# Expert tables loaded in pairs of tiles, and the gates of PEER spilled by 32 tokens

## The chip, the cores and the metric

One core of a Trainium2 chip runs the whole layer. The metric is the device time in us of one execution; several executions give a median. The engines are PE (matmul), DVE (vector), ACT (scalar), POOL (GpSimd, which issues the indirect gathers), SP (which issues nearly all other DMAs) and 16 DMA engines that all queues share.

## The reference

A layer with 512 tokens of 1024 channels: attention with a sliding window and a causal pooling branch, merged by gates, then PEER, a retrieval over 16384 single-neuron experts, then a last RMSNorm. What the change touches is PEER:

```python
q = (xc @ w_query).reshape(c, 8, 2, 128)
sc = einsum('chpd,hpkd->chpk', q, sub_keys)           # 16 score sets of 128 keys
sv, si = lax.top_k(sc, 16)
cand = sv[:, :, 0, :, None] + sv[:, :, 1, None, :]    # 256 candidates a head
fv, fi = lax.top_k(cand.reshape(c, 8, 256), 16)
idx = take_along_axis(cidx, fi, -1); g = softmax(fv)  # expert number = 128*i + j
a = gelu(einsum('chkd,cd->chk', u_tab[idx], xc))
out = einsum('chk,chkd->cd', g * a, v_tab[idx])
```

All arithmetic is in float32.

## The kernel before

**Two ways for PEER.** Block 0 of 128 tokens (GB) gathers its rows of the u and v tables with indirect DMAs, two for each of the 128 choices of a token (`gather`, L735): POOL issues, DVE forms the dot product (L745) or adds the row (L749). The other 384 tokens (three blocks, ND) go through both tables densely: for each of 128 tiles n of 128 experts, `u_part` (L604) forms gelu(u tile times tokens), a gate matrix says how much each token wants of each expert, and `v_mm` (L630) adds gates times v tile into PSUM. Of the first block of those, 32 tokens (CT) have their u side by gathers too (`few`, L716), so a u tile is multiplied with 352 tokens.

**Precision.** Each matmul is three: ACT casts a float32 tile to `wh` (L121, or `vh`), DVE forms the rest `wl` = raw - wh (L113, or `vl`), and PE multiplies hi by hi, hi by lo and lo by hi (L108 to L110). So each weight tile of 512 KB passes DMA, ACT, DVE, PE. The raw tiles `wr` have RAW = 3 buffers, filled by SP in program order; a load waits until DVE has done the `low` that last read its buffer. In the dense phase the v tiles use `vr`, also 3 buffers.

**Stages** (us in the profile of before). Mixing and its projections run to 356. `scores` (L446) to 470: 16 tiles of `w_query`, of 24 matmuls 128x512 each, `match` after each, and after four of them a block of `top16` on DVE, 80 instructions (L486 to L494) for 4 projections of 4 blocks of tokens; after every fourth projection comes one `u_part`. DVE's order in this stage, `top16` against `low`, is made by a scheduler. Then the route to 978: `part()` (L825) runs u tiles ahead of time, 104 in all, of which 14 results stay in SBUF (RES) and 90 are written to `ahead`; beside them run by credits (R_A, G_A a part) the top 16 of the candidates (`select`, L496), the one-hot work and the gathers. `onehot` (L556) makes the gates: a batch is 8 tokens; `ohj` is made on ACT for 3 batches of 4 (8 times L574 and once L575) and on DVE for the fourth (L577), `ohi` on DVE (L580, L581), PE multiplies them (L590), ACT copies the product to `gs` (L591), and after TG = 16 tokens `gs` goes to `spill` in HBM in one DMA of 1 MB (L593). There are three spreads of 16 batches: one at 658 to 742, two at 797 to 978. Six more parts (TAIL) cover the first loads of the dense phase.

**The dense phase** (`dense`, L674) takes 128 iterations, from 1004 to 1657. Each loads a v tile (512 KB, L120), reloads the 176 KB result of a u tile (`gar`, L619), and in four of every eight iterations a quarter of the gates of the next eight tiles (`gt`, L627, 384 KB in runs of NI * TG * 4 = 512 bytes). ACT and DVE make `wh`, `wl` and `vh`, `vl`; PE does 18 matmuls 128x512. The last 24 iterations, from 1434, do their u part in place: a u tile more and 24 matmuls 128x352. The remaining gather rows are spread over the phase, at a rate G_B / G_V three times higher an iteration in the last 24. The order of PE, DVE and ACT is as the program is written here; SP's and POOL's DMAs follow by their waits.

Of the kernel before, what the change touches and what calls it, by code (L numbers as in the profile page):

```python
# [19 lines left out]
P = 128  # L20
# [20 lines left out]
GB = 0  # L41
# [5 lines left out]
TG = 16  # L47
# [3 lines left out]
G_A = 1.0  # L51
# [7 lines left out]
RES = 14  # L59
SC = 1.4  # L60
RAW, ROWS, WB = 3, 4, 3
OHN, OHA = 4, 3


class Layer:
# [49 lines left out]
    def weights(self, src, pool=None, tag="w", late=False):  # L115
        k = WB if pool is None else 2
        pool = pool or self.w
        raw, hi, lo = (pool.tile([P, D], t, name=tag + n, tag=tag + n, bufs=b)
                       for n, t, b in (("r", F32, RAW), ("h", F32R, k), ("l", F32R, k)))
        self.nc.sync.dma_start(out=raw, in_=src)  # L120
        self.nc.scalar.copy(hi, raw)  # L121
# [277 lines left out]
    def residual(self, wp, tp, mg, xn2, nat):  # L399
# [5 lines left out]
        def load(k):  # L405
            raw = self.w.tile([P, D], F32, name="wr", tag="wr", bufs=RAW)
# [197 lines left out]
    def u_part(self, n, w, xn2, keep=False):  # L604
        ps = self.project(w, xn2, slice(DB * P + CT, DB * P + TD))
        if keep and n < RES:
            ga = self.held[n] = self.ga.tile([P, TU], F32, name=f"gk{n}", bufs=1)
# [3 lines left out]
        if keep and n >= RES:  # L611
            self.nc.sync.dma_start(out=self.ahead[n], in_=ga)
        return ga

    def reload(self, n):
        if n < RES:
            return self.held.pop(n)
# [37 lines left out]
    def v_load(self, m):  # L655
        self.vs[m], low = self.weights(self.a["v_experts"][m * P:(m + 1) * P, :], self.dp, "v", late=True)
        return low
# [16 lines left out]
    def dense(self, ahead, xn2, acc, fetch):  # L674
        us = {}

        def u_load(m):
            if ahead <= m < NKEY:
                us[m] = self.weights(self.a["u_blocks"][m])
# [101 lines left out]
    def run(self):  # L781
        nc, tc, a = self.nc, self.tc, self.a
        xn2 = self.pair(self.x, "x")
        with tc.tile_pool(name="merged", bufs=1) as self.m:
# [4 lines left out]
            nat = {GB: self.c.tile([P, D], F32, name="natg")}  # L789
            self.cp = self.pool("few", 1, side="right")  # L790
            self.natc = self.cp.tile([P, D], F32, name="natc")
# [4 lines left out]
        with tc.tile_pool(name="route", bufs=1, reuse_waits="tile") as tp:  # L796
            subk = tp.tile([P, 16, P], F32, name="subk")
            nc.scalar.dma_start(out=subk, in_=a["sub_keys"])

# [23 lines left out]
            self.held = {}  # L823
# [10 lines left out]
            for i, _ in enumerate(self.scores(xn2, tp, sv, si, subk)):  # L834
                if i % U_S == U_S - 1:
                    part()
# [11 lines left out]
        with tc.tile_pool(name="dense", bufs=2, reuse_waits="tile") as self.dp:  # L848
# [13 lines left out]
            for c in range(ND):  # L862
                hb = dp.tile([P, D], F32, name="hb", tag="vr", bufs=RAW)
# [68 lines left out]
```

## Time and profile before

| | us |
|---|---|
| three runs | 1670.08, 1674.9 (median), 1680.72 |
| profiled execution, its own time | 1678.21 |
| its span in the profile | 1676.4 |
| busy in the span: PE, DVE, ACT, POOL | 1578.3, 1285.2, 803.8, 371.4 |
| DMA | 417.83 MB, mean 249 GB/s |

PE is busy for 94% of the span, but the stages have different limits, so the window rows by stage say more than this mean. A matmul's busy time overlaps its neighbours', so the distance between starts is the better measure of PE's pace. [...]

### The profile page before, as it was taken

To read this page: it belongs to the slowest core of one execution; us is meant where nothing else is said; L and a number is where in the kernel's file an instruction comes from. 1 tells how busy PE (TensorE), PEld (TensorE's weight loads), DVE (VectorE), ACT (ScalarE), POOL (GpSimd) and SP (SyncE) were. 2 spreads that over 40 slices of the span, in tenths; PEclk is the share of its full clock that TensorE was granted. 3 is DMA by queue.
4 is the path that set the end of the run, shared out by engine and by line. 5 is a ranking of instruction groups with operands and counts; after the bars stand their busy time and mean duration, and the time that the engine had idled before them with its cause. 6 is when DMAs were issued, how large, how long until landed. Compare 5 with 4: busy or idle time off the path is not lost.

```text
span 1676.4 us, 23543 instructions
## 1 busy us (share of the span) xinstructions
PE 1578.3 (94%) x8389; PEld 1370.7 (82%) x8389; DVE 1285.2 (77%) x2379; ACT 803.8 (48%) x1434; POOL 371.4 (22%) x302
## 2 busy tenths in 40 slices
PE   7999999999998989899888989999999999999997
PEld 6777788888898989889888887777877778787876
DVE  4676434437899999789888858888887888788887
ACT  4655533333343436983998943333333333332334
POOL 0000000000001243223322213243333333254550
PEclk9999999999999989999999999999999999999999
DMA  6211222532236888878878799999999999999994
GB/s 213 65 62 64 75 95 94 184 117 93 84 114 224 276 293 294 283 259 266 297 274 288 260 303 371 335 354 365 366 364 336 342 356 361 331 332 358 333 334 154
DMA packets 173175, 417.83 MB, mean 249 GB/s; under 512 B 15616, under 2 KB 88064, under 8 KB 169856
## 3 DMA queue, kind: packets, MB, share of 16 engines
q1 hardware_dynamic: 130576, 262.65, 45.3%
q0 software_dynamic: 41728, 151.05, 26.0%
q10 hardware_dynamic: 752, 2.62, 0.4%
q8 instruction: 66, 1.08, 0.3%
q14 instruction: 53, 0.43, 0.1%
HBM read 370.12 MB, written 45.06 MB: 248 GB/s over the span
## 4 chain that ended last, share of the span: by engine, by line
PE 41%; issue 23%; DMA 11%; ACT 9%; DVE 8%; POOL 7%; SPq 1%; POOLq 0%; DVEq 0%; ACTq 0%
PE mm L108 7%; PE mm L109 7%; PE mm L110 7%; POOL row L712 7%; PE acc L109 4%; PE acc L108 4%; PE acc L110 4%; DMA row<-v_experts,ei 3%; DMA vr<-v_experts 3%; ACT ohj L574 3%; ACT gs L591 2%; DVE wl L113 2%; ACT wh L121 1%; PE ho L108 1%; PE ho L110 1%
## 5 line engine op out<-in xcount | busy, mean ns | idle before, releaser
L108 PE MATMUL mm<-xh,wh 128*128 128x352 f32 (+2 forms) x1424 | 491.2, 345 | 11.3 <-ACT ga L610 8.0
L110 PE MATMUL mm<-xh,wl 128*128 128x352 f32 (+2 forms) x1424 | 483.7, 340 | 6.2 <-DVE wl L113 6.2
L109 PE MATMUL mm<-xl,wh 128*128 128x352 f32 (+2 forms) x1424 | 483.6, 340 | 0.7 <-DVE xl L113 0.7
L712 POOL DMA_INDIRECT row<-u_experts,ei x128 | 158.3, 1237 | 847.3 <-ACT ga L610 528.3
L113 DVE TENSOR_TENSOR wl<-wr,wh 128x1024 fp32r<-128x1024 f32 x187 | 228.3, 1222 | 143.8 <-ACT wh L121 138.9
L108 PE MATMUL acc<-vh,wh 128*128 128x512 f32 x768 | 303.5, 395 | 19.7 <-ACT wh L650 12.8
L121 ACT CAST wh<-wr 128x1024 fp32r<-128x1024 f32 x187 | 195.6, 1046 | 245.6 <-PE mm L109 188.8
L109 PE MATMUL acc<-vl,wh 128*128 128x512 f32 x768 | 304.0, 396 | 7.7 <-DVE vl L113 7.4
L110 PE MATMUL acc<-vh,wl 128*128 128x512 f32 x768 | 302.9, 394 | 0.0
L108 PEld LDWEIGHTS mm<-xh,wh 128*128 128x128 f32 x1424 | 271.0, 190 | 32.1 <-ACT ga L610 10.3
L110 PEld LDWEIGHTS mm<-xh,wl 128*128 128x128 f32 x1424 | 270.8, 190 | 21.6 <-DVE wl L113 7.8
L109 PEld LDWEIGHTS mm<-xl,wh 128*128 128x128 f32 x1424 | 271.2, 190 | 13.8 <-DVE xl L113 1.1
L650 ACT CAST wh<-wf 128x384 fp32r<-128x384 f32 x128 | 65.7, 514 | 363.0 <-PE acc L109 174.0
L712 POOL DMA_INDIRECT row<-v_experts,ei x128 | 163.7, 1279 | 308.1 <-DVE hg L749 268.4
L113 DVE TENSOR_TENSOR vl<-vr,vh 128x1024 fp32r<-128x1024 f32 x128 | 156.5, 1223 | 69.1 <-ACT vh L121 63.2
L108 PEld LDWEIGHTS acc<-vh,wh 128*128 128x128 f32 x768 | 145.3, 189 | 55.9 <-ACT wh L650 16.6
L109 PEld LDWEIGHTS acc<-vl,wh 128*128 128x128 f32 x768 | 145.4, 189 | 45.4 <-DVE vl L113 16.7
L110 PEld LDWEIGHTS acc<-vh,wl 128*128 128x128 f32 x768 | 145.3, 189 | 34.3 <-DVE wl L113 4.4
L749 DVE SCALAR_TENSOR_TENSOR hg<-row,act,hg 128x1024 f32<-128x1024 f32 x128 | 163.9, 1281 | 4.0 <-DMA row<-v_experts,ei 3.5
L745 DVE SCALAR_TENSOR_TENSOR row<-row,natg 128x1024 f32<-128x1024 f32 x128 | 156.0, 1219 | 6.8 <-DMA row<-u_experts,ei 6.8
L121 ACT CAST vh<-vr 128x1024 fp32r<-128x1024 f32 x128 | 134.0, 1047 | 52.6 <-DMA vr<-v_experts 48.1
L590 PE MATMUL pg<-ohi,ohj 128*128 128x128 f32 x768 | 96.5, 279 | 27.5 <-ACT ohj L575 24.2
(188 smaller groups left out, 1743.7 us busy)
## 6 DMA issues: line engine op xcount, KB each, us to landing
wr<-u_blocks SPq DMA_DIRECT2D x128, 512.0 KB
vr<-v_experts SPq DMA_DIRECT2D x128, 512.0 KB
spill<-gs SPq DMA_DIRECT2D x24, 1024.0 KB
gt<-spill SPq DMA_DIRECT2D x64, 384.0 KB
ahead<-ga SPq DMA_DIRECT2D x90, 176.0 KB
gar<-ahead SPq DMA_DIRECT2D x90, 176.0 KB
wr<-w_in SPq DMA_DIRECT2D x30, 512.0 KB
wr<-w_query SPq DMA_DIRECT2D x16, 512.0 KB
```

The lines of the kernel that those rows point to most:

```text
L108: mm(out, lhsT=l[0], rhs=r[0], start=first, stop=False)
L109: mm(out, lhsT=l[0], rhs=r[1], start=False, stop=False)
L110: mm(out, lhsT=l[1], rhs=r[0], start=False, stop=last)
L113: self.lowered = self.nc.vector.tensor_tensor(lo, src, hi.bitcast(F32), op=ALU.subtract).ins
L121: self.nc.scalar.copy(hi, raw)
L574: nc.scalar.activation(ohj[:, z, :], self.iota, AF.Abs, bias=tr[:, 1, u + z:u + z + 1])
L590: nc.tensor.matmul(pg[:, z, :], lhsT=ohj[:, z, :], rhs=ohi[:, z, :], start=True, stop=True)
L591: nc.scalar.copy(gs[0][:, :, t0:t0 + 8].rearrange("p i t -> p t i"), pg)
L650: nc.scalar.copy(wh, wf)
L712: self.nc.gpsimd.indirect_dma_start(out=t, out_offset=None, in_=tab, in_offset=bass.IndirectOffsetOnAxis(ap=ei[:, s:s + 1], axis=0))
L745: nc.vector.scalar_tensor_tensor(u, u, 1.0, xn2, op0=ALU.mult, op1=ALU.mult, accum_out=act[:, s:s + 1])
L749: nc.vector.scalar_tensor_tensor(z, v, act[:, s:s + 1], z, op0=ALU.mult, op1=ALU.add)
```

## The change

- **Tables in pairs.** Two neighbouring u tiles, and two v tiles, come in one DMA of 1 MB, 8192 contiguous bytes a partition instead of 4096 (`u_tile`, `v_tile`). For v, a pair holds the experts with j even and odd next to each other, so `indices` maps an expert to another tile and row: 3 tensor_scalar and 1 tensor_tensor instead of 2 tensor_scalar. The u table comes to the kernel as `u_pairs`, laid out so.
- **Buffers.** `wr` has 2 buffers of 8 KB a partition instead of 3 of 4 KB, for every stream; a single tile (`w_in`, `w_o`, `w_query`) fills half of one. `vr` likewise has 2 pairs.
- **Gates.** TG is 32: `gs` goes to HBM every 4 batches in 2 MB, and `gt` comes back in runs of 1024 bytes, in the same 64 loads of 384 KB.
- **One-hot.** `ohj` is made on ACT for every second batch (OHN, OHA = 2, 1): L574 issues 192 instead of 288, L575 24 instead of 36, L577 24 instead of 12.
- **Smaller things.** G_A is 1.1: 62 gather rows of block 0 are asked for ahead of the dense phase instead of 51, so 194 instead of 205 are left for it. KEEP and HELD keep 2 + 12 u results in SBUF, as many as RES, but those of the u parts 2 and 3 go to `ahead`. `score`'s tiles are in a pool of their own, and `natg` is in another pool.

The instructions of PE keep their number (7819); 104 parts ahead, 90 of them written to `ahead`, and 24 in the dense phase stand in both.

The core of the diff:

```diff
-TG = 16
+TG = 32
-G_A = 1.0
+G_A = 1.1
-RES = 14
+KEEP = 2
+HELD = 12
-RAW, ROWS, WB = 3, 4, 3
-OHN, OHA = 4, 3
+RAW, ROWS, WB = 2, 4, 3
+OHN, OHA = 2, 1
...
+    def raw(self):
+        return self.w.tile([P, 2, D], F32, name="wr", tag="wr", bufs=RAW)
+
+    def weights(self, src):
+        raw = self.raw()[:, 0, :]
         self.nc.sync.dma_start(out=raw, in_=src)
+        return self.halves(raw, self.w, "w", WB)
...
+    def u_tile(self, m):
+        if m % 2 == 0:
+            self.two_u = self.raw()
+            self.nc.sync.dma_start(out=self.two_u.rearrange("p j d -> p (j d)"), in_=self.a["u_pairs"][m // 2])
+        return self.halves(self.two_u[:, m % 2, :], self.w, "w", WB)
+
+    def v_tile(self, m):
+        if m % 2 == 0:
+            self.two_v = self.dp.tile([P, 2, D], F32, name="vr", tag="vr", bufs=2)
+            self.nc.sync.dma_start(out=self.two_v.rearrange("p j d -> p (j d)"), in_=self.a["v_pairs"][m // 2])
+        return self.halves(self.two_v[:, m % 2, :], self.dp, "v", 2, late=True)
...
-        v.tensor_scalar(ij[:, 0, :], ei, 7, None, op0=ALU.arith_shift_right)
-        v.tensor_scalar(ij[:, 1, :], ei, NKEY - 1, None, op0=ALU.bitwise_and)
+        v.tensor_scalar(ij[:, 1, :], ei, 1, None, op0=ALU.bitwise_and)
+        v.tensor_scalar(ij[:, 0, :], ei, 8, 1, op0=ALU.arith_shift_right, op1=ALU.logical_shift_left)
+        v.tensor_tensor(ij[:, 0, :], ij[:, 0, :], ij[:, 1, :], op=ALU.bitwise_or)
+        v.tensor_scalar(ij[:, 1, :], ei, 1, NKEY - 1, op0=ALU.arith_shift_right, op1=ALU.bitwise_and)
...
             def part():
                 nonlocal ahead
                 with tc.high_priority(HP):
-                    w = self.weights(a["u_blocks"][ahead])
+                    w = self.u_tile(ahead)
...
+    a["v_pairs"] = a["v_experts"].rearrange("(m p j) d -> m p (j d)", p=P, j=2)
```

The buffers change the order in which SP loads the tiles of `scores`. SP before, from the end of the `w_o` projection (names: `wr` a raw tile, `hb`, `hspill` and `natc` blocks of the residual):

```order
L120 DMA wr_2981<-w_query 128x1024
L427 DMA hspill<-hb_2686 128x1024
L120 DMA wr_3106<-w_query 128x1024
L120 DMA wr_3145<-w_query 128x1024
L120 DMA wr_3182<-w_query 128x1024
L120 DMA wr_3218<-u_blocks 128x1024
L120 DMA wr_3252<-w_query 128x1024
```

SP in the change, from the load of the first pair of u tiles:

```order
L135 DMA wr_2950<-u_pairs 128x2048
L444 DMA hspill<-hb_2686 128x1024
L121 DMA wr_2984<-w_query 128x1024
L121 DMA wr_3109<-w_query 128x1024
L121 DMA wr_3148<-w_query 128x1024
L121 DMA wr_3185<-w_query 128x1024
L121 DMA wr_3253<-w_query 128x1024
```

The pair is loaded ahead of tile 4 of `w_query`, and its second half is read only by the u part that stands after tile 7. Until then its buffer is held, and the tiles 4 to 7 (rows 3 to 6) share the other one. The same comes again with the second pair and the tiles 12 to 15.

DVE's order moves with it. DVE before, in the first block of `top16` (`sv`, `si` values and indices, `sc` scores):

```order
L486 MAX sv_2734<-sc 128x8 x4
L488 MAX_INDEX si_2738<-sv_2734,sc 128x8 x4
L490 MATCH_REPLACE sc<-sv_2734,sc 128x128
L113 TENSOR_TENSOR wl<-wr,wh 128x1024
L490 MATCH_REPLACE sc<-sv_2734,sc 128x128 x3
L492 MAX sv_2734<-sc 128x8 x4
```

DVE in the change, the last of four equal parts of that block and what stands behind it:

```order
L503 MAX sv_2734<-sc 128x8 x4
L505 MAX_INDEX si_2738<-sv_2734,sc 128x8 x4
L507 MATCH_REPLACE sc<-sv_2734,sc 128x128 x4
L509 MAX sv_2734<-sc 128x8 x4
L511 MAX_INDEX si_2738<-sv_2734,sc 128x8 x4
L114 TENSOR_TENSOR wl<-wr,wh 128x1024 x6
```

The rest `wl` of tile 7, which stood inside the first block, now stands behind all 80 instructions of it, as the first of six; the third block has no `wl` inside either, where it had two.

SP in the dense phase before, one group of gates:

```order
L120 DMA vr<-v_experts 128x1024
L627 DMA gt<-spill 128x6x128
L619 DMA gar<-ahead 128x352
L627 DMA gt<-spill 128x6x128
L120 DMA vr<-v_experts 128x1024
L619 DMA gar<-ahead 128x352
L627 DMA gt<-spill 128x6x128
L120 DMA vr<-v_experts 128x1024
L619 DMA gar<-ahead 128x352
L627 DMA gt<-spill 128x6x128
L120 DMA vr<-v_experts 128x1024
```

and in the change, the same group:

```order
L141 DMA vr<-v_experts 128x2048
L639 DMA gar<-ahead 128x352
L647 DMA gt<-spill 128x3x256
L639 DMA gar<-ahead 128x352
L647 DMA gt<-spill 128x3x256 x2
L141 DMA vr<-v_experts 128x2048
L639 DMA gar<-ahead 128x352
L647 DMA gt<-spill 128x3x256
L639 DMA gar<-ahead 128x352
L141 DMA vr<-v_experts 128x2048
```

Before, at most two gate loads stood ahead of a v load of 512 KB; now three stand ahead of a v load of 1 MB.

## Rows read from the trace of the kernel before

**Rows 1.** The head of the page: the span of the profiled execution.

```profile
span 1676.4 us, 23543 instructions
```

**Rows 2.** Windows, one row for each stage of the program that the prediction prices: start and end in us, length, then the busy us and number of instructions of PE, PEld, DVE, ACT and POOL, the granted TensorE clock, the DMA share and GB/s.

```profile
356.00:470.00 114.00, 113.55 (x619) 99.86 (x619) 80.44 (x405) 37.88 (x56) 0.00 (x0) 1.00 0.27 93
...
470.00:658.00 188.00, 175.87 (x1061) 173.35 (x1060) 180.20 (x577) 74.28 (x109) 42.24 (x36) 0.96 0.73 245
...
658.00:742.00 84.00, 73.86 (x523) 70.67 (x523) 70.32 (x104) 78.42 (x138) 19.79 (x13) 1.00 0.78 272
...
797.00:978.00 181.00, 160.97 (x1132) 155.78 (x1132) 149.11 (x145) 171.79 (x301) 43.87 (x28) 1.00 0.81 277
...
1004.00:1434.00 430.00, 415.66 (x1789) 335.14 (x1788) 351.90 (x477) 159.89 (x302) 138.24 (x118) 0.99 1.01 355
...
1434.00:1657.00 223.00, 209.84 (x1053) 181.31 (x1053) 188.23 (x229) 77.41 (x137) 99.93 (x80) 0.99 0.91 319
```

**Rows 3.** Timeline of DVE through `scores`: start, duration, line, operation, out<-in, shapes, and in brackets the idle time before it. L486 is the first instruction of a block of `top16`, L113 the rest of a weight tile, L504 the first instruction of `select`.

```profile
387.85 0.87 DVE L486 MAX8 sv<-sc 128x8 f32<-128x128 f32 x4
...
394.61 1.21 DVE L113 TENSOR_TENSOR wl<-wr,wh 128x1024 fp32r<-128x1024 f32 x1
...
407.70 2.34 DVE L113 TENSOR_TENSOR wl<-wr,wh 128x1024 fp32r<-128x1024 f32 x2
...
446.38 0.87 DVE L486 MAX8 sv<-sc 128x8 f32<-128x128 f32 x4
...
470.26 0.87 DVE L486 MAX8 sv<-sc 128x8 f32<-128x128 f32 x4
...
494.65 0.27 DVE L504 CAST sf<-si 128x256 f32<-128x256 uint32 x1
```

**Rows 4.** Timeline of PE in `scores`: the first matmul behind the products of a score block that reads the rest (`wl`) of a weight tile.

```profile
399.76 0.39 PE L110 MATMUL mm<-xh,wl 128*128 128x512 f32 x1
```

**Rows 5.** The chain that ended last: pieces of it that are DMAs, with start us, duration us, and what was moved. `wr<-u_blocks` and `vr<-v_experts` are 512 KB each, `spill<-gs` 1 MB.

```profile
776.09 5.35 DMA wr<-u_blocks
...
904.85 3.48 DMA wr<-u_blocks
...
978.30 5.80 DMA spill<-gs
...
1071.97 11.32 DMA vr<-v_experts
```

**Rows 6.** Windows of 4 us on both sides of a stall of PE in the route, columns as in rows 2.

```profile
600.00:604.00 4.00, 3.77 (x24) 3.48 (x22) 2.55 (x12) 1.17 (x1) 0.94 (x1) 1.00 1.03 411
...
616.00:620.00 4.00, 4.00 (x15) 4.00 (x14) 4.00 (x6) 0.00 (x0) 1.68 (x1) 0.50 0.87 263
```

**Rows 7.** Groups of instructions in the one-hot stretch from 797 to 978 us: line, engine, operation, out<-in, shapes, count, busy us in all, mean ns of one, idle time before them and its releaser; and the summary of the tile `gs` in the same stretch, with the first and the last start of its 32 copies.

```profile
L591 ACT COPY gs<-pg 128x1024 f32<-128x1024 f32 x32 | 63.0, 1996 | 6.9 <-PE pg L590 6.9
...
L574 ACT ACTIVATE ohj<-iota,tr 128x128 f32<-128x128 f32 x192 | 59.5, 401 | 4.5 <-DVE tr L564 4.5
...
L575 ACT ACTIVATE ohj<-ohj 128x1024 f32<-128x1024 f32 x24 | 25.6, 1065 | 0.3
...
L577 DVE TENSOR_TENSOR ohj<-iota,tr 128x1024 f32<-128x1024 f32 x8 | 9.8, 1222 | 6.9 <-PE pg L590 6.9
...
L749 DVE SCALAR_TENSOR_TENSOR hg<-row,act,hg 128x1024 f32<-128x1024 f32 x14 | 17.9, 1279 | 0.0
...
L591 ACT COPY gs<-pg x32: 1929/1997/2057, 807.3 to 976.3; 128x1024 f32<-128x1024 f32 x32
```

**Rows 8.** DMA queues by window: packets, MB, and the time of the packets as a share of 16 DMA engines over the window. First 350 to 375 us, where q1 moves 4096-byte packets of `w_query` tiles but for 64 of 2 KB or less and q10 moves `sub_keys` in 8192-byte packets.

```profile
q1 hardware_dynamic: 576, 2.10, 24.0%
...
q10 hardware_dynamic: 144, 1.05, 10.8%
```

**Rows 9.** The same view from 990 to 996 us, where q1 moves mostly the 512-byte runs of `gt`; then 1004 to 1434 us, with the number of issues of `vr` and `gt` under it; then 1434 to 1657 us. q0 is the queue of the indirect gathers.

```profile
q1 hardware_dynamic: 2545, 1.30, 80.4%
...
q1 hardware_dynamic: 67304, 89.47, 60.6%
q0 software_dynamic: 17295, 62.96, 39.9%
...
vr<-v_experts SPq DMA_DIRECT2D x100, 512.0 KB
...
gt<-spill SPq DMA_DIRECT2D x49, 384.0 KB
...
q0 software_dynamic: 11520, 41.95, 53.9%
```

**Rows 10.** GB/s in 40 equal slices of the window from 0 to 25 us, in which the loads of x and `w_in` run with nothing beside them (4096-byte packets).

```profile
GB/s 0 0 52 190 328 262 249 367 328 413 420 419 420 419 420 419 349 325 179 5 40 76 120 178 268 357 403 413 426 420 419 275 203 79 236 354 243 0 92 328
```

**Rows 11.** Timeline of PE in the two parts of the dense phase: 128x512 products of the v table, 17 products from the first row to the second, and 128x352 products of a u tile, 23 from the third row to the fourth.

```profile
1099.76 0.39 PE L109 MATMUL acc<-vl,wh 128*128 128x512 f32 x1
...
1103.61 0.39 PE L108 MATMUL acc<-vh,wh 128*128 128x512 f32 x1
...
1502.01 0.33 PE L108 MATMUL mm<-xh,wh 128*128 128x352 f32 x1
...
1505.67 0.32 PE L110 MATMUL mm<-xh,wl 128*128 128x352 f32 x1
```

**Rows 12.** Waits from 1004 to 1434 us: who waited <- for what: us in all, times, longest us.

```profile
ACT vh L121 <- DMA vr<-v_experts: 40.9, 21, 5.5
```

More of the change, by code (lines that the diff above doesn't have):

```diff
@@ L113, in low, with halves @@
         self.lowered = self.nc.vector.tensor_tensor(lo, src, hi.bitcast(F32), op=ALU.subtract).ins
[L115 to L119, printed above, removed]
+    def raw(self):
+        return self.w.tile([P, 2, D], F32, name="wr", tag="wr", bufs=RAW)
+    def weights(self, src):
+        raw = self.raw()[:, 0, :]
         self.nc.sync.dma_start(out=raw, in_=src)
+        return self.halves(raw, self.w, "w", WB)
+    def halves(self, raw, pool, tag, bufs, late=False):
+        hi, lo = (pool.tile([P, D], F32R, name=tag + n, tag=tag + n, bufs=bufs) for n in "hl")
         self.nc.scalar.copy(hi, raw)
@@ L405, in load @@
         def load(k):
-            raw = self.w.tile([P, D], F32, name="wr", tag="wr", bufs=RAW)
+            raw = self.raw()[:, 0, :]
             nc.sync.dma_start(out=raw, in_=self.a["w_o"][k])
@@ L605, in u_part @@
         ps = self.project(w, xn2, slice(DB * P + CT, DB * P + TD))
-        if keep and n < RES:
-            ga = self.held[n] = self.ga.tile([P, TU], F32, name=f"gk{n}", bufs=1)
+        if keep and self.room:
+            self.room -= 1
+            ga = self.held[n] = self.home.tile([P, TU], F32, name=f"gk{n}", bufs=1)
         else:
@@ L610, in u_part @@
         self.nc.scalar.activation(ga, ps, AF.Gelu)
-        if keep and n >= RES:
+        if keep and n not in self.held:
             self.nc.sync.dma_start(out=self.ahead[n], in_=ga)
@@ L615, in reload @@
     def reload(self, n):
-        if n < RES:
+        if n in self.held:
             return self.held.pop(n)
@@ L655, in v_load @@
     def v_load(self, m):
-        self.vs[m], low = self.weights(self.a["v_experts"][m * P:(m + 1) * P, :], self.dp, "v", late=True)
+        self.vs[m], low = self.v_tile(m)
         return low
@@ L678, in u_load @@
             if ahead <= m < NKEY:
-                us[m] = self.weights(self.a["u_blocks"][m])
+                us[m] = self.u_tile(m)
         def rate(m):
@@ L788, in run @@
             self.psum(self.ctx, "ps3", 3)
-            nat = {GB: self.c.tile([P, D], F32, name="natg")}
             self.cp = self.pool("few", 1, side="right")
+            nat = {GB: self.cp.tile([P, D], F32, name="natg")}
             self.natc = self.cp.tile([P, D], F32, name="natc")
@@ L795, in run @@
         self.rows = self.pool("rows", ROWS, reuse_waits="tile")
-        with tc.tile_pool(name="route", bufs=1, reuse_waits="tile") as tp:
-            subk = tp.tile([P, 16, P], F32, name="subk")
-            nc.scalar.dma_start(out=subk, in_=a["sub_keys"])
+        with tc.tile_pool(name="route", bufs=1, side="right", reuse_waits="tile") as tp:
             def pool(b):
@@ L822, in run @@
             ahead = 0
-            self.held = {}
+            self.held, self.home, self.room = {}, self.ga, KEEP
             def part():
@@ L832, in part @@
                 return after
-            for i, _ in enumerate(self.scores(xn2, tp, sv, si, subk)):
-                if i % U_S == U_S - 1:
-                    part()
+            with tc.tile_pool(name="score", bufs=1, side="right", reuse_waits="tile") as sp:
+                subk = sp.tile([P, 16, P], F32, name="subk")
+                nc.scalar.dma_start(out=subk, in_=a["sub_keys"])
+                for i, _ in enumerate(self.scores(xn2, sp, sv, si, subk)):
+                    if i % U_S == U_S - 1:
+                        part()
+            self.home, self.room = self.pool("held", 1, reuse_waits="tile"), HELD
             first = Background(self.select(tp, sv[GB], si[GB], ei[GB], gw[GB]))
@@ L862, in run @@
             for c in range(ND):
-                hb = dp.tile([P, D], F32, name="hb", tag="vr", bufs=RAW)
+                hb = dp.tile([P, 2, D], F32, name="hb", tag="vr", bufs=2)[:, 0, :]
                 nc.sync.dma_start(out=hb, in_=self.hspill[c])
```

2 lines of the change are left out of this document (1 added, 1 removed).

## The prediction

> **What bounds the kernel now.** I read the table of windows by stage first, since a mean over the span mixes unlike stages. The sum is made against the profiled execution's own time of 1678.2 us (span 1676.4 [rows 1]); the median of the three runs is 3.3 us lower. Five stages are touched [rows 2]. In `scores` (356 to 470) PE is busy 113.55 of 114 us: PE bounds it. From 470 to 658 DVE is busy 180.2 of 188 us: DVE bounds the selection. In the one-hot stretch from 797 to 978 ACT is busiest, 171.79 of 181 us, with PE at 160.97 and DVE at 149.11; 658 to 742 reads alike (78.42 of 84, then 73.86 and 70.32). In the dense phase to 1434 the DMA share is 1.01, PE 415.66 of 430; from 1434 to 1657 the share is .91.
>
> For the dense phase I also take PE's pace. Seventeen products of 128x512 take 3.85 us from start to start, so eighteen, an iteration, 4.08; 23 products of a u tile take 3.66 us, so 24 take 3.82 [rows 11]. The 1789 matmuls to 1434 are 99.4 iterations, 405 us of 430: about 25 us are lost, 2.0 in each group of eight iterations. The 1053 from there on are 25.1 iterations of 7.90 us, 198 of 223: another 25 lost. That is all that faster transfers can give back there. In the first part the losses are ACT's: 40.9 us of waiting for `vr` in 21 waits [rows 12].
>
> **Scores: the loss.** Raw tiles have two buffers now, and a pair of u tiles holds one of them while four tiles of `w_query` go through the other, each load behind DVE's `low` of the tile ahead. A load takes about 3.5 us (chain pieces: 3.48 and 5.35 [rows 5]). DVE's order fell in with this: `low` of tile 7 ran at 394.61, inside the first block of `top16`, which lasted from 387.85 to 407.70 [rows 3]; now it stands behind the block. Without that one instruction (1.13 us of spacing, from 1.21 busy) the block takes 18.7 us, so the `low` runs at 406.6 and ends at 407.8. PE wants it where it read `wl` at 399.76 [rows 4]: 7 to 8 us of stall, and behind it the whole queue of PE. Then tiles 8 to 11 follow from late loads, and the second block of `top16`, which needs tile 11, starts about 7 us late. Tiles 12 to 14 each take load, cast and `low` through one buffer, 3.5 + 1.07 (as the ACT operation of the same shape, L575 [rows 7]) + 1.2 us, and start only when the second block is done: I get the third block at 457 instead of 446.38. Tile 15's `low` stands behind its 18.7 us, at 476.5; PE's pass, 24 x .2265 = 5.4 us, and ACT's copies come after it, so the fourth block starts at about 486.6 instead of 470.26. It holds two `low`s where before it held five (24.39 us to 494.65), so `select` starts at 507.7: **+13 us**. What could cover it is gone: the stage behind it is DVE's. Bounds: 8, if the first stall alone stays, and 20, if the stalls also cost clock; behind an earlier stall in the route the granted clock fell from 1.00 to .50, which is 1.2 GHz of the two levels [rows 6].
>
> Elsewhere two raw buffers mean at most a wait in the mixing, where tiles are asked for two ahead: **+1** (0 to 4).
>
> **More rows in the route.** Eleven more gathered rows come before the dense phase. A row costs DVE 1.28 us [rows 7]; some 6.5 of the eleven fall in the selection, bound by DVE, 8 us; most of the four others and all of POOL's issues lie beside PE. Part of the eight fills DVE's gaps: **+5** (0 to 9).
>
> **One-hot: the gain.** A batch costs ACT 24 of 32 times (59.5 + 25.6) / 24 = 3.55 us for `ohj`, and DVE the other times 1.22 [rows 7]. With 16 of 32 on each, ACT falls by 8 x 3.55 = 28.4 to 143.4 us in 797 to 978, DVE rises by 9.8 to 158.9, PE stays at 161. In 658 to 742 ACT falls by 14.2, DVE rises by 4.9 to 75.2. The bounds go from 172 to 161 and from 78.4 to 75.2, and if the stretches shrank to their busiest engine it would be 20 + 8.8, so 28 us in all. Batches come every (976.3 - 807.3) / 31 = 5.45 us now; 161 us over 32 batches would be 5.03. But PE and DVE would then stand within 2% of each other, and neither covers the other's waits, so I take half: **-14** (-28 to 0, the latter if PE's waits for ACT only turn into waits for DVE). The new integer instructions on 128x128 are few: four more a block, well under 1 us each, counted in this range.
>
> **The joint.** The last spill is 2 MB; one of 1 MB took 5.80 us on the chain [rows 5], and the first gate loads wait for it: **+1** (-1 to +5), since six u parts lie beside it.
>
> **Dense phase.** Priced in time of 16 engines. A packet of 4096 bytes took 24.0% x 25 x 16 / 512 = 187 ns (512 such packets make the 2.10 MB), one of 8192 took 10.8% x 25 x 16 / 128 = 337 ns, so 169 for 4 KB [rows 8]: 100 v loads of 128 packets save 128 x 100 x 18 / 16 = 14 us (0 if the rate in a full queue doesn't move). A run of 512 bytes took 80.4% x 6 x 16 / 2545 = 30.3 ns [rows 9]; 49 loads of 768 are 71 us. At the 4 KB rate per byte it would be 23.4 ns, or 55 us: no row has 1024 bytes, so I take the middle, -8 (-16 to 0). Six rows fewer: 62.96 MB of gathers are 120 rows, 39.9% of 430 us, 1.43 us each, -9. In all -31 of some 434 us, which would put the DMA under PE's 405. As the losses come in bursts behind the gate loads, I give back two thirds of the 25: **-17** (-25 to -5). In the last part 4.6 rows less at 53.9% x 223 / 80 = 1.50 us are -7, pairs -7, gates -1; two thirds of 15: **-10** (-24 to 0).
>
> On the gates a rule speaks against this. By the Trainium skill (DMA: Bandwidth & Descriptors, Specifications) a transfer runs at line rate from 512 bytes on, so doubling the runs would give nothing there; by it the term of -8 is 0. The row of 30.3 ns against 23.4 for the same bytes at 4 KB disagrees, if the mix of that window is not the reason.
>
> **Sum:** 1 + 13 + 5 - 14 + 1 - 17 - 10 = -21, so 1657 against 1678.2, and **1654** against the median.
>
> **Rivals.**
> *The serial loads are hidden and the dense phase reaches PE's pace.* The loads of tiles 4 to 7 may be early enough, as PE's order has been moved too, and then `scores` costs nothing; and the first dense part gives 25 instead of 17. 1654 - 13 - 8 = 1633. Against it: the `low` of tile 7 is behind the block by program order whatever the loads do. Chance .15.
> *Packets change nothing.* In a full queue the memory sets the rate; then only the rows saved count, 9/31 of the first term (-5) and 7/15 of the second (-5): 1654 + 12 + 5 = 1671. For it: 355 GB/s at a share of 1.01 in the dense phase. Against: 413 to 420 GB/s with 4096-byte packets at the start [rows 10]. Chance .21. The Trainium skill (HBM Reference, Specifications (TRN2)) gives a core about 358 GB/s with both cores of a pair streaming, and about 425 alone; here one core runs, and the rows at the start agree with the second figure, so by it the dense phase is not yet at its rate.
> *Slower: pairs land late.* The buffer of an even tile is freed no earlier than before, about two iterations (8.2 us) ahead of ACT's cast, but its load is 1 MB, has to land whole, and stands behind three gate loads instead of two. A load of 512 KB in this phase took 11.32 us already where it was on the chain [rows 5]. If a pair lands 2 us later than that in each of the 12.4 groups, the loss doubles to 50: +25 instead of -17, so 1654 + 42 = 1696. It decides from a landing of some 13 us on. Against: the odd tiles need no load of their own any more, and the total of bytes falls. Chance .14.
>
> **How the numbers follow.** Forecast .46, rivals .15, .21, .14, anything else .04. The forecast's own range is 1643 to 1668 (loss of `scores` 8 to 20, one-hot -20 to -8, dense -5 either way, not all at once). The range of 8 in 10 runs from the first rival's 1633 to short of the third, 1632 to 1684. A measurement tells about 1% from no change: 1658 and 1692. Of the forecast .30 lies below 1658, all of the first rival, .01 of the rest: faster .46. Slower: .11 of the third rival and .02: .13. Same .41.
>
> **What would show it.** In the profile of the changed kernel: PE idle some 7 us at about 400 and some 11 at about 466, waiting for DVE's `wl`, and `select`'s first cast at about 507; ACT near 143 us and DVE near 159 between the first and last `gs` of the last two spreads, `gs` copies 5.0 to 5.3 us apart; a v pair's 8192-byte packet at or under 340 ns and gate runs of 1024 bytes under 55 ns; ACT's wait for `vr` under 20 us in the first dense part. I am wrong if `select` starts before 500 or if ACT's wait for `vr` has grown beyond 41 us.

## The result, and the profile after

The changed kernel takes 1691.68 us (median of 4 runs, 1690.6 to 1701.12), the kernel before 1674.0 (4 runs beside it): ratio 1.0124, 95% interval [1.0082, 1.0166]. It is slower by about 1.2%, above the range of the prediction and on the other side of its forecast. The profiled execution took 1692.68 us.

Where the time went is best seen by the starts of a few instructions that both kernels have. Stage lengths in us, each the difference of two such starts in the two traces:

| from .. to | before | after | difference | forecast |
|---|---|---|---|---|
| start .. first cast of `select` | 494.7 | 512.3 | +17.6 | +14 |
| .. first `gs` (three selections) | 166.0 | 179.9 | +13.9 | +5, with the gap below |
| .. 16th `gs` (first spread) | 81.2 | 76.6 | -4.6 | -14, with the next spreads |
| .. 17th `gs` (the gap, fourth selection) | 65.4 | 73.1 | +7.7 | |
| .. 48th `gs` (two spreads) | 169.0 | 157.8 | -11.2 | |
| .. first dense product | 27.9 | 28.9 | +1.0 | +1 |
| .. first u part in the dense phase | 446.2 | 434.1 | -12.1 | -17 |
| .. last dense product | 215.6 | 210.2 | -5.4 | -10 |
| .. end | 10.4 | 18.0 | +7.6 | 0 |

The differences add up to the 14.5 us between the spans. The forecasts add up to -21, so the miss is 35.5 us: 16.6 in the selections and the gap, 9.5 in the dense phase, 7.6 at the end, 3.6 in `scores`, and -1.8 in the one-hot work.

In `scores` PE stalls near the places that the forecast named. Waits of the changed kernel from 356 to 512 us (who waited <- for what: us in all, times, longest):

```profile
ACT wh L126 <- DMA wr<-w_query: 23.1, 4, 12.3
...
ACT wh L126 <- DMA wr<-u_pairs: 14.1, 1, 14.1
PE mm L111 <- DVE wl L114: 13.7, 2, 7.8
...
PE mm L109 <- ACT gk L630: 6.4, 1, 6.4
```

The 13.7 us are two stalls of PE behind DVE's `wl`: 5.84 us from 402.1 on (forecast some 7 at 400) and 7.82 us from 470.1 on (forecast some 11 at 466). DVE's timeline there (start, duration, line, operation, in brackets the idle time before it):

```profile
406.67 2.33 DVE L114 TENSOR_TENSOR wl<-wr,wh 128x1024 fp32r<-128x1024 f32 x2
...
426.01 0.86 DVE L503 MAX8 sv<-sc 128x8 f32<-128x128 f32 x4
...
445.84 1.22 DVE L114 TENSOR_TENSOR wl<-wr,wh 128x1024 fp32r<-128x1024 f32 x1
451.34 1.23 DVE L114 TENSOR_TENSOR wl<-wr,wh 128x1024 fp32r<-128x1024 f32 x1 [4.27 <-ACT wh L126]
456.84 1.23 DVE L114 TENSOR_TENSOR wl<-wr,wh 128x1024 fp32r<-128x1024 f32 x1 [4.28 <-ACT wh L126]
457.99 0.87 DVE L503 MAX8 sv<-sc 128x8 f32<-128x128 f32 x4
...
491.37 0.86 DVE L503 MAX8 sv<-sc 128x8 f32<-128x128 f32 x4
```

The serial buffer shows in the three `wl` that start 5.5 us apart: DVE is idle for 4.3 us ahead of the second and of the third, while load and cast run. Tile 7's rest comes at 406.67 (394.61 before [rows 3]), the third block of `top16` at 457.99 (446.38 before), the fourth at 491.37 (470.26 before). The stalls cost clock too; two windows, the first over 8 us behind the second stall, columns as in [rows 2]:

```profile
477.90:485.90 8.00, 7.94 (x24) 6.38 (x25) 2.36 (x3) 1.32 (x2) 0.00 (x0) 0.65 0.69 262
470.00:508.00 38.00, 23.78 (x116) 21.80 (x116) 29.27 (x152) 8.84 (x13) 0.00 (x0) 0.78 0.33 121
```

What was not foreseen stands on ACT right there. ACT's timeline of the changed kernel:

```profile
497.36 0.59 ACT L482 COPY sc<-pss 128x512 f32<-128x512 f32 x1 [2.46 <-DVE si L511]
497.84 1.05 ACT L126 CAST wh<-wr 128x1024 fp32r<-128x1024 f32 x1
503.16 0.59 ACT L482 COPY sc<-pss 128x512 f32<-128x512 f32 x1 [4.28 <-DVE si L511]
503.65 0.83 ACT L630 ACTIVATE gk<-mm 128x352 f32<-128x352 f32 x2
```

Two gelus, of the parts 4 and 5, stand back to back behind the last copy of the scores, while PE's next product waits 6.4 us for them (the row above): both PSUM buffers of the parts are full.

The one-hot work did what was said of it. Windows of the changed kernel, from the 17th to the last `gs` and over the first spread:

```profile
841.90:999.70 157.80, 150.70 (x1077) 147.54 (x1076) 148.96 (x147) 142.58 (x215) 55.81 (x29) 1.00 0.81 296
692.20:768.80 76.60, 74.07 (x529) 73.15 (x529) 72.54 (x102) 69.16 (x102) 21.99 (x13) 1.00 0.78 276
```

PE is busiest now, then DVE, then ACT: `gs` copies are 157.8 / 31 = 5.09 us apart instead of 5.45. ACT's 142.58 us are the 143 that were forecast; DVE's 148.96 are under the 159.

In the dense phase ACT waits less for v tiles. The wait from 1028 to 1462 us, to be held against [rows 12]:

```profile
ACT vh L126 <- DMA vr<-v_experts: 15.1, 9, 4.3
```

At the end DVE's timeline has a hole:

```profile
1670.60 2.65 DVE L792 TENSOR_TENSOR hb<-acc,hb 128x512 f32<-128x512 f32 x4 [3.24 <-PE acc L111]
...
1683.39 1.29 DVE L792 TENSOR_TENSOR hb<-acc,hb 128x512 f32<-128x512 f32 x2 [4.59 <-DMA hb<-hspill]
```

The last residual block `hb` is added 12.8 us behind the first two. It is loaded into the v tiles' buffers, of which there are now two, so its load can only be issued when another block is done.

### The profile page after: what moved, and what is told of

It reads as the page before. It is cut to its first block, busy times and chain, and to the rows that moved or that the text cites. A ratio compares the mean times of both kernels' runs of the same rounds, so it can differ in the third digit from the quotient of the medians.

```text
span 1690.9 us, 22978 instructions
## 1 busy us (share of the span) xinstructions
PE 1579.4 (93%) x8389; PEld 1382.5 (82%) x8389; DVE 1302.2 (77%) x2397; ACT 772.9 (46%) x1326; POOL 377.2 (22%) x302
## 4 chain that ended last, share of the span: by engine, by line
PE 23%; issue 15%; DVE 9%; DMA 6%; ACT 5%; POOL 5%; SPq 1%; POOLq 0%; DVEq 0%; ACTq 0%
PE acc L110 5%; POOL row L732 5%; PE acc L109 5%; PE acc L111 4%; PE pg L609 3%; PE mm L109 2%; PE mm L110 2%; PE mm L111 2%; DMA vr<-v_experts 2%; DVE wl L114 2%; DMA row<-v_experts,ei 2%; ACT gs L610 2%; ACT ohj L593 1%; DVE row L747 1%; DVE ohi L599 1%
## 5 line engine op out<-in xcount | busy, mean ns | idle before, releaser
L111 PE MATMUL mm<-xh,wl 128*128 128x352 f32 (+2 forms) x1424 | 486.1, 342 | 13.7 <-DVE wl L114 13.7
L111 PEld LDWEIGHTS mm<-xh,wl 128*128 128x128 f32 x1424 | 272.5, 191 | 28.9 <-DVE wl L114 14.5
L732 POOL DMA_INDIRECT row<-v_experts,ei x128 | 167.3, 1307 | 281.8 <-DVE hg L769 258.5
L610 ACT COPY gs<-pg 128x1024 f32<-128x1024 f32 x48 | 98.9, 2086 | 12.5 <-PE pg L609 12.5
```

The lines of the kernel that those rows point to most:

```text
L111: mm(out, lhsT=l[1], rhs=r[0], start=False, stop=last)
L610: nc.scalar.copy(gs[0][:, :, t0:t0 + 8].rearrange("p i t -> p t i"), pg)
L732: self.nc.gpsimd.indirect_dma_start(out=t, out_offset=None, in_=tab, in_offset=bass.IndirectOffsetOnAxis(ap=ei[:, s:s + 1], axis=0))
```

## Experiments

The theory after the result: (1) a pair of u tiles holds one of two raw buffers in `scores`; (2) the pool of held results is opened in memory that the score tiles gave up, and stops ACT; (3) more rows in the route cost DVE more than they spare later; (4) `hb` waits for a buffer; against them (5) half the `ohj` on DVE, and (6) pairs and gate runs, give something back. The main rival: the dense phase, short of DMA, takes up what the route gives or loses, and pairs arriving in lumps are what lengthens the route. Each time is a median with the kernel before on the same chip beside it. Its own median was 1674.0 us beside the changed kernel, 1673.45 beside u4_single, hb_halves, rows_as_before and onehot_alone, 1677.01 beside u4_heldlate_hb, u4_heldlate_hb_rows, v_single and tg16, and 1674.71 beside the last three runs; so across these groups the ratios are compared, and the changed kernel's is 1.0124. To compare stages I use one table for all kernels, the start in us of the first matmul of u part 4, 10, 47, 59 and 103, then the first and the last dense product and the end of the span, worked out from each trace:

```
kernel                 4     10     47     59     103   first   last    end
before             468.8  491.7  653.1  739.1  1000.2  1004.2 1666.0 1676.4
after              489.9  531.9  691.9  768.6  1018.5  1028.6 1672.9 1690.9
u4_single          469.3  510.5  669.4  745.9   996.8  1007.3 1650.3 1668.5
hb_halves          491.4  533.2  693.4  769.8  1019.9  1030.6 1678.5 1689.1
rows_as_before     488.8  530.6  682.8  763.5  1006.8  1016.0 1668.0 1685.9
onehot_alone       468.5  491.5  652.8  734.6   979.6   983.4 1648.8 1659.2
u4_heldlate_hb     468.6  491.6  664.1  740.8   992.4  1003.0 1649.9 1660.6
u4_heldlate_hb_rows 469.9 492.9  662.2  738.8   981.1   989.7 1641.7 1652.3
v_single           489.0  530.8  690.4  767.2  1020.7  1027.1 1672.7 1683.7
tg16               489.6  512.8  683.7  760.0  1009.7  1013.5 1661.0 1678.5
rows_fewer         469.5  492.4  650.4  730.0   969.4   976.7 1665.9 1676.5
all_u_single       467.4  490.3  660.2  736.8   978.0   985.4 1633.6 1644.3
```

The changed kernel, u4_single, hb_halves and u4_heldlate_hb have the same program from the first to the last dense product and take 643.0 to 647.9 us there, so a difference under 5 us in that phase shows nothing. Parts are a better measure than `select`'s cast: at the cast the kernel before had begun its 11th part, the changed one its 8th.

**Run u4_single.** On the changed kernel:

```diff
     def u_tile(self, m):
+        if m < 4:
+            raw = self.raw()[:, 0, :]
+            self.nc.sync.dma_start(out=raw, in_=self.a["u_pairs"][m // 2, :, m % 2 * D:(m % 2 + 1) * D])
+            return self.halves(raw, self.w, "w", WB)
         if m % 2 == 0:
```

> The changed kernel, but the first four u tiles, those of the scores stage, are loaded one by one as before; all later pairs stay. Theory (a pair holds one of two raw buffers, so four w_query tiles go through the other): DVE's order is again that of before, PE's stalls of 5.84, 7.82 and 6.39 us go, select's first cast comes at 495 to 498 instead of 512.3, and since the selection behind it is DVE's the gain reaches the end: about 1676 instead of 1691. Rival (the dense phase, short of DMA, takes up whatever the route gives): the cast moves, but the last product of the dense phase stays within 5 us of 1672.9, time 1686 or more.

1671.6 us, ratio to before 0.9992 [0.9978, 1.0006], some 20 us under the changed kernel, 22 by the ratios. Part 4 starts at 469.3 instead of 489.9, and at the end of the span 22.4 us are gained. The theory holds and the rival falls: what is lost in `scores` reaches the end. But part 10 still starts 18.8 us later than before, so there is a second cause at the head of the route. DVE's timeline of this run shows 20 us without a `wl` there, on both sides of `select`'s first cast:

```profile
479.65 1.22 DVE L114 TENSOR_TENSOR wl<-wr,wh 128x1024 fp32r<-128x1024 f32 x1
491.75 0.28 DVE L525 CAST sf<-si 128x256 f32<-128x256 uint32 x1
499.98 1.22 DVE L114 TENSOR_TENSOR wl<-wr,wh 128x1024 fp32r<-128x1024 f32 x1
```

**Run hb_halves.** On the changed kernel:

```diff
-                hb = dp.tile([P, 2, D], F32, name="hb", tag="vr", bufs=2)[:, 0, :]
+                if c != 1:
+                    two = dp.tile([P, 2, D], F32, name="hb", tag="vr", bufs=2)
+                hb = two[:, c % 2, :]
```

> The changed kernel, but two of the three hb blocks of the end share one pair buffer of vr, so no hb load waits for a block that is being finished. Theory: the tail from the last product to the end falls from 18.0 to about 10.4 us, time 1684. Rival (the tail is long for another reason, such as the output's DMAs): the third add stays at 12 us behind the first two, time 1691.

1687.09 us, ratio 1.0083 [1.0053, 1.0114]. The tail from the last product to the end is 10.6 us instead of 18.0; the third add follows the first two at once:

```profile
1676.16 2.65 DVE L792 TENSOR_TENSOR hb<-acc,hb 128x512 f32<-128x512 f32 x4 [3.25 <-PE acc L111]
...
1678.88 1.29 DVE L792 TENSOR_TENSOR hb<-acc,hb 128x512 f32<-128x512 f32 x2
```

The theory holds. The span fell by only 1.8 us, since this execution's earlier stages were 5.6 us longer; that says how far two executions differ.

**Run rows_as_before.** On the changed kernel:

```diff
-G_A = 1.1
+G_A = 1.0
```

> The changed kernel with G_A 1.0, so 51 rows asked for ahead of the dense phase and not 62. Theory (the rows alone make the selections longer): from select's first cast to the first gs 171 us instead of 179.9, the gap between the 16th and the 17th gs 66 instead of 73, and 11 rows more in the dense phase cost 8 to 12 us there, so the time moves by less than 6. Rival (pairs arriving in lumps make the selections longer, not the rows): both stretches stay within 2 us of 179.9 and 73, the dense phase still loses, and the time is 5 to 12 us longer, about 1700.

1688.34 us, ratio 1.0104 [1.0077, 1.013]. The gap between the spreads is 66.6 us (theory 66), the three selections 177.2 (theory 171, rival 179.9), the dense phase 652.0 instead of 644.3, the time 3.3 us less. So the gap was the rows', but of the 13.9 us of the selections only 2.7.

**Run onehot_alone.** On the kernel before:

```diff
-OHN, OHA = 4, 3
+OHN, OHA = 2, 1
```

> The kernel before with half of the ohj batches on DVE instead of a quarter, nothing else. Theory (ACT bounds these stretches): 16 batches in 77 us instead of 81.2 and 32 in 158 instead of 169.0, as in the changed kernel, time 1674 - 15 = 1659. Rival (spills of 2 MB and pairs gave that gain): 81 and 167 or more, time 1672 or more.

1657.81 us, ratio 0.9914 [0.9887, 0.994]. The windows of this run over the same two stretches as above:

```profile
801.10:959.50 158.40, 150.66 (x1076) 147.52 (x1075) 147.94 (x144) 140.30 (x215) 46.30 (x27) 1.00 0.86 300
659.70:734.90 75.20, 69.82 (x501) 67.78 (x500) 69.44 (x85) 65.61 (x101) 18.70 (x12) 1.00 0.83 280
```

158.4 and 75.2 us: the gain is this edit's alone, and by itself it makes the kernel before faster by 0.9%.

**Run u4_heldlate_hb.** The edits of u4_single and hb_halves, and:

```diff
-        if keep and self.room:
+        if keep and self.room and not 2 <= n < 12:
```

> The changed kernel with three edits: the first four u tiles one by one (as in u4_single), hb in halves (as in hb_halves), and the held results are those of the parts 0, 1 and 12 to 23, so that no part up to 11 writes into the pool that is opened when the tiles of scores are given up; 14 are held as before. In u4_single part 10 still started at 510.5 us against 491.7 before. Theory (ACT's gelu of part 4 has to wait for the last copies of the score tiles, whose memory it is given, and so PE and DVE's lows wait): part 10 starts at 491 to 495, the time is 1671.6 - 16 - 8 = 1648. Rival (u pairs of 1 MB through two raw buffers make the start of the route late): part 10 stays at 508 or later and only the tail is gained, 1664.

1659.61 us, ratio 0.9879 [0.9849, 0.9909]. Part 10 starts at 491.6, as in the kernel before, and ACT does each gelu between the copies of the scores:

```profile
476.09 0.59 ACT L486 COPY sc<-pss 128x512 f32<-128x512 f32 x1 [2.05 <-DVE si L515]
476.57 1.05 ACT L126 CAST wh<-wr 128x1024 fp32r<-128x1024 f32 x1
477.52 0.47 ACT L634 ACTIVATE ga<-mm 128x352 f32<-128x352 f32 x1
481.89 0.58 ACT L486 COPY sc<-pss 128x512 f32<-128x512 f32 x1 [3.91 <-DVE si L515]
482.38 1.05 ACT L126 CAST wh<-wr 128x1024 fp32r<-128x1024 f32 x1
483.32 0.47 ACT L634 ACTIVATE ga<-mm 128x352 f32<-128x352 f32 x1
```

So the mechanism is shown. Its price at the end is not: in these two profiles, of 18.9 us against u4_single at part 10, 5.3 are left at part 47, 4.3 at the first dense product and 0.4 at the last. The medians differ by 12.0, of which the tail is 7.6, so 4 remain. But the two runs had different chips beside them; by the ratios (0.9992 and 0.9879) 19 us lie between them, and 11 remain. So 0 to 11 us reach the end, and 1648, the sum of the theory, was too low by 5 to 12. How part of it is made up in this pair shows from 520 to 640 us, where PE is busy all 120 us in u4_single and 112.3 here. One window of u4_single, then the same of this run (columns as in [rows 2]):

```profile
520.00:560.00 40.00, 40.00 (x242) 40.00 (x241) 35.22 (x124) 15.70 (x22) 12.64 (x10) 1.00 0.76 267
```

```profile
520.00:560.00 40.00, 35.39 (x218) 34.23 (x217) 37.17 (x129) 15.25 (x21) 14.61 (x11) 1.00 0.71 255
```

**Run u4_heldlate_hb_rows.** The same with G_A 1.0:

```diff
-G_A = 1.1
+G_A = 1.0
```

> The kernel of u4_heldlate_hb with G_A 1.0, 51 rows ahead of the dense phase instead of 62. Theory (rows cost DVE in the route about what they spare the dense phase): first product of the dense phase 9 to 12 us earlier, the dense phase 8 to 10 longer, time within 4 us of u4_heldlate_hb. Rival (with the stalls gone the route hides the rows): the dense phase starts within 3 us of the other and the time is 6 us or more longer.

1655.61 us, ratio 0.9866 [0.9825, 0.9906], 4.0 under its neighbour. The first dense product is 13.3 us earlier, the dense phase 652.0 instead of 646.9: ten rows (53 instead of 63 used ahead, counted in the traces) cost the route 13.3 us and spare the dense phase 5.1, hardly more than executions differ by. The theory holds on the time, with both parts off in size. The three selections take 166.7 us here and the gap 64.3, together 231.0, against 231.4 in the kernel before and 253.0 in the changed one: the held results and the rows account for all that these stages lost.

**Run v_single.** On the changed kernel (`hb` gets three buffers as well):

```diff
-        if m % 2 == 0:
-            self.two_v = self.dp.tile([P, 2, D], F32, name="vr", tag="vr", bufs=2)
-            self.nc.sync.dma_start(out=self.two_v.rearrange("p j d -> p (j d)"), in_=self.a["v_pairs"][m // 2])
-        return self.halves(self.two_v[:, m % 2, :], self.dp, "v", 2, late=True)
+        raw = self.dp.tile([P, D], F32, name="vr", tag="vr", bufs=3)
+        self.nc.sync.dma_start(out=raw, in_=self.a["v_pairs"][m // 2, :, m % 2 * D:(m % 2 + 1) * D])
+        return self.halves(raw, self.dp, "v", 2, late=True)
```

> The changed kernel with v tiles loaded one by one in 4096-byte runs into three buffers, as before, from the new order of experts; hb has its three buffers too. Theory (8192-byte packets are cheaper in a full queue, 327 ns against two of 173, and a pair lands ahead of its odd tile): first to last product of the dense phase 650 to 653 us instead of 644.3, ACT's wait for vr back above 30 us, tail 10.4, time 1691 + 7 - 8 = 1690. Rival (the dense gain is the rows' and the gates' alone): 643 to 646, ACT's wait as in the changed kernel, time 1683.

1688.19 us, ratio 1.0062 [1.0041, 1.0083], 10 us under the changed kernel by the ratios, of which the tail is 7. Dense phase 645.6 us instead of 644.3, tail 11.0. The rival holds on the dense phase: v pairs are worth 1.3 us there, which two executions can differ by. The time alone does not decide (it lies nearer the theory's 1690, but its chip's kernel before is 3 us slower), and on ACT's wait for `vr` (from 1010 to 1440 us) the rival was wrong: it is larger than with pairs, but the phase is hardly longer for it:

```profile
ACT vh L126 <- DMA vr<-v_experts: 27.6, 15, 7.5
```

**Run tg16.** On the changed kernel:

```diff
-TG = 32
+TG = 16
```

> The changed kernel with TG 16: spills of 1 MB and gate runs of 512 bytes again. Theory (two runs of 512 bytes take 60 ns where one of 1024 took 49): the dense phase 4 to 7 us longer than 644.3; and as gs takes half the room, the held results no longer lie where the score tiles were, so part 10 starts about 16 us earlier than 531.9; time about 1680. Rival (runs of 512 bytes are as good): dense phase within 2 us of 644.3, time 1674. If part 10 stays at 530, the held results' memory is not the cause of the late start.

1687.55 us, ratio 1.0069 [1.0048, 1.009]. The dense phase is 647.5, 3.2 us longer, which is within what two executions differ by, so the price of the runs stays open. Part 10 starts at 512.8 instead of 531.9, as the theory of the held results' memory said, though TG has nothing to do with the parts: only `gs` is half as large, and the rest lies elsewhere. ACT's timeline has the gelus between the copies again:

```profile
494.43 0.46 ACT L630 ACTIVATE gk<-mm 128x352 f32<-128x352 f32 x1
496.99 0.59 ACT L482 COPY sc<-pss 128x512 f32<-128x512 f32 x1 [2.10 <-DVE si L511]
...
498.42 0.47 ACT L630 ACTIVATE gk<-mm 128x352 f32<-128x352 f32 x1
502.80 0.59 ACT L482 COPY sc<-pss 128x512 f32<-128x512 f32 x1 [3.91 <-DVE si L511]
```

Of the 19.1 us at part 10, 15.1 are there at the first dense product, far more than the 4.3 of u4_heldlate_hb (2.6 of the 15.1 lie behind the last `gs`, where the smaller spill may count); in time it is 4 us by the medians and 9 by the ratios. The time is some 7 us above the forecast of 1680; the 8 runs spread from 1680.3, which is the profiled one, to 1694.87.

**Run rows_fewer.** On u4_heldlate_hb, `G_A = 0.8`.

> The kernel of u4_heldlate_hb with G_A 0.8 (0.8 of the credit a part for gathers, so some 17 rows fewer than at 1.0 are asked for ahead of the dense phase). Theory (a row costs the route about 1.2 us of DVE, and spares the dense phase 0.5 to 0.7): first product of the dense phase about 15 us earlier than 989.7, dense phase 9 to 12 us longer than 652.0, time 3 to 6 us under 1655.6. Rival (from 1.0 down the route is no longer DVE's): first product less than 5 us earlier, dense phase longer all the same, time 5 us or more above 1655.6.

1673.19 us, ratio 0.998 [0.9961, 0.9999]. Both theories fall. The route is still DVE's: first dense product 13.0 us earlier, 16 rows fewer. But the dense phase is 689.2 us instead of 652.0: 2.3 us a row, against 0.5 between G_A 1.0 and 1.1. The profiled execution was the slowest of 12, 5 us above their median; by the medians (17.6 us longer, with 13.0 gained ahead of the phase) it is 1.9 a row. The last part alone, with 7 rows more, went from 215.3 to 236.5. Waits of this run from 1429 to 1666 us, then of u4_heldlate_hb_rows from 1426 to 1642:

```profile
ACT wh L674 <- DVE wf L673: 140.4, 22, 11.1
...
PE acc L109 <- ACT wh L674: 27.5, 14, 5.3
```

```profile
ACT wh L674 <- DVE wf L673: 120.7, 22, 7.8
...
PE acc L109 <- ACT wh L674: 13.6, 12, 2.4
```

ACT waits longer for DVE's gates' product (`wf`), and PE twice as long behind ACT. That the rows ahead of it on DVE are what delays it is my reading of the order. So the cost of a row in the dense phase rises steeply below 1.0; of 1.1, 1.0 and 0.8, 1.0 has the lowest median.

**Run all_u_single.** On u4_heldlate_hb_rows every u tile by itself, from `u_pairs`, with three raw buffers:

```diff
-        return self.w.tile([P, 2, D], F32, name="wr", tag="wr", bufs=RAW)
+        return self.w.tile([P, 1, D], F32, name="wr", tag="wr", bufs=3)
...
-            self.nc.sync.dma_start(out=self.two_u.rearrange("p j d -> p (j d)"), in_=self.a["u_pairs"][m // 2])
-        return self.halves(self.two_u[:, m % 2, :], self.w, "w", WB)
+        raw = self.raw()[:, 0, :]
+        self.nc.sync.dma_start(out=raw, in_=self.a["u_pairs"][m // 2, :, m % 2 * D:(m % 2 + 1) * D])
+        return self.halves(raw, self.w, "w", WB)
```

> The kernel of u4_heldlate_hb_rows with every u tile loaded by itself, in 4096-byte runs, into three raw buffers of 4 KB; v pairs, gates of 1024 bytes, hb in halves stay. Theory (u pairs bring nothing: PE, DVE and ACT bound the route): first product of the dense phase within 4 us of 989.7 and the same time, 1655 +- 5. Rival (pairs through two buffers hold up the later route, in which part 47 started 9 us later than in the kernel before): part 47 at 653 to 656 instead of 662, time 1647 or less.

1648.98 us, ratio 0.986 [0.9829, 0.9891]; u4_heldlate_hb_rows had 0.9866. Part 47 stays at 660.2, first dense product 985.4, 4.3 us earlier, of which 2.5 are there at part 4 already. By the ratios it is 1 us faster, by the medians 6.6, more than the theory's 5, but part 47 is not where the rival had it. So the theory holds in the main: u pairs bring nothing, and may cost a few us. It is the fastest kernel of the study, 1.4% under the kernel before, and has the one-hot edit, the long gate runs and v pairs without the four losses. What delays part 47 by 7 to 9 us in both was not tried.

**Run onehot_alone_again.** The kernel of onehot_alone, on the same chip as the two above.

> The kernel of onehot_alone once more, beside the two others on one chip. If it is the one-hot work alone that makes this change worth anything, it is within 5 us of them; if the gates of 1024 bytes and the v pairs add to it, the faster of the two others is 6 us or more below it.

1657.28 us, ratio 0.9897 [0.9867, 0.9927]. all_u_single is 8.3 us below it, so gates and v pairs, with what comes along with them (separate pools, `hb` in halves), are worth some 8 us beside the one-hot edit; the intervals overlap.

## Why the prediction was wrong

**Scores: mechanism right, size a little short.** The term was +13 within 8 to 20. The stage gave +17.6 to `select`'s cast, and undoing it gave back 20.6 us at part 4, 20 by the medians, at the upper end of that range. The schedule worked out there was near: tile 7's rest at 406.6 (measured 406.67), the third block at 457 (457.99), the fourth at 486.6 (491.37); on the way 457 and 18.7 make 475.7, not the 476.5 that stands there, and nothing hangs on it. Of the 4.8 us missing in the last, 2.6 are clock, which the sum left to the upper bound: behind the second stall 23 matmuls of tile 15 took 7.8 us (477.96 to 485.8) where the pace of .2265 makes 5.2, at a granted clock of .65 over that window (above): up to 483.2 the starts are .43 us apart, which is 512 columns at 1.2 GHz, the lower of the two levels, and then .23. From the end of that pass to the block it is 5.5 us where the working had 3.5, since PE does the 24 products of a u part (485.77 to 489.1) before it scores tile 15.

**Selections: the step that failed.** The prediction had +5 for the rows and nothing else; with the gap they are 21.6 us longer. Two things were missed. The rows cost more: the gap between the spreads grew by 7.7 us, and fell by 6.5 when the rows were taken back; ten rows cost the route 13.3, since it has no gaps in DVE for them, where I had counted on POOL and some of the rows lying beside PE. And KEEP and HELD were taken as a renaming, "as many as RES": the new pool is opened when the score tiles are given up, so part 4's gelu comes behind their last copies in ACT's order, PE's PSUM buffers fill up, and DVE's `wl`s, placed behind, come after the whole fourth block. It is 18.8 us at part 10 and 8.1 in the three selections (178.0 in u4_single, 169.9 in u4_heldlate_hb). With both undone, in u4_heldlate_hb_rows, the stages are back at 231.0 us, against 231.4 before; u4_single alone leaves 252.0.

**The end: a term left out.** I gave `vr` two buffers in the dense phase and didn't ask who else uses them. `hb` does, three times: +7.6 us.

**One-hot: right.** -14 forecast, -15.8 measured in the changed kernel, and -17 by itself. That it took half of 28 was a guess, and it came out. The new integer instructions are two more a block (four for two), not four.

**Dense phase: two thirds of the forecast.** -27 forecast, -17.5 measured. The rows' share is about 7.7 (rows_as_before). Undoing v pairs alone costs 1.3, undoing the long gate runs alone 3.2, neither clear of what two executions differ by; both together were not tried on this kernel. With the rows as before the dense phase is 652.0 here against 661.8 before, and 665.4 in onehot_alone, which has these rows and the one-hot edit, so both together are near 10 to 13; 648.2 in all_u_single against 665.2 in onehot_alone_again would make it 17. The prices of packets, in ns per packet of one DMA engine, means over the first dense part worked out from the packet records of both traces:

```
bytes     512   1024   4096 (v)   8192 (v pair)
ns         30     49       173        327
```

The 8192-byte packet saves 19 ns of 346, 5.5%, not the 10% that the quiet window gave [rows 8]: for 100 v loads that is 7.6 us of 16 engines, where 14 were priced. The 1024-byte run saves 11 ns of 60, 13 us for 49 loads where I took 8. By the Trainium skill (DMA: Bandwidth & Descriptors, Specifications) nothing was to be had above 512 bytes; the trace disagrees, 17 bytes a ns at 512, 21 at 1024, 24 at 4096. The rule there to batch DMAs to 1 MiB or more (Bandwidth), given with loads issued from GpSimd, is not borne out as a gain here, where SP issues them: v pairs of 1 MB are worth 1.3 us by v_single, u pairs nothing by all_u_single, and a pair that holds one of two buffers in `scores` cost 20.

**The rivals.** The third, pairs landing late, forecast 1696 and was the nearest in time, by luck: ACT's wait for `vr` fell from 40.9 to 15.1 us. The second, that packets change nothing, was near the truth for the v pairs in time, though not for the packets themselves. The two signs that I set for being wrong, `select` before 500 and ACT's wait above 41 us, both stayed away (512.3 and 15.1): they watched terms that were right, and none watched the selections or the end.

**What stays open.** The effects as measured one by one, +20 to +22 for scores, +7.6 for the end, +3 to +8 for rows net, 0 to +11 for the held results, -14 to -17 for one-hot and -10 to -17 for pairs and gates, add up to between -3 and +25; the changed kernel is 17.7 slower by the medians. So the sum agrees, but it is too wide to say whether the effects add, or whether an effect is missing. How much of the held results' loss reaches the end is the widest term.

## What to carry to other kernels

When transfers are made larger, ask who else takes buffers from the same pool: a double tile that is read half now and half later holds its buffer for both, and the neighbours go through what is left, one by one. A result that is moved to a pool opened over freed memory gets the old tenants' waits, and what stands behind it in ACT's order gets them as well (18.8 us at part 10). Change one thing at a time where the gain is (here two thirds of it, 17 of 26 us, were two numbers in one line), and take the start of a repeated unit of work, not a stage's border, as the clock when two schedules are compared.

## What the runs showed that was not expected

A loss of 18.8 us at the head of the route was down to 4.3 at the first dense product in one pair of kernels (u4_single and u4_heldlate_hb), while one of 20.6 us a little earlier went through in full. My reading is that the first only delayed parts that PE could catch up with, and the second put off DVE's own work, the blocks of `top16`; no run was made that tells this apart, and tg16 does not fit it well, as there 15.1 of 19.1 us were still gained at the first dense product. And the price of a gathered row in the dense phase went from 0.5 us (63 to 53 rows taken ahead) to 2 us or so (53 to 37).
